# The last projection of the second layer over 33 attention steps in place of 53, and the first output projection over 97 in place of 77

## The chip, the core and the metric

The kernel runs on one core of one Trainium2 chip. The metric is the device time of one execution in microseconds (us). A core has five engines with a queue of instructions each: TensorE (PE, matrix products), VectorE (DVE), ScalarE (ACT), GpSimd (POOL) and SyncE (SP, which here only issues transfers). An engine takes its instructions in the order in which the program lists them, so an instruction whose inputs are late holds everything behind it on that engine. Transfers are issued by SP and ACT, and run on 16 DMA engines.

## The reference, cut to what matters

The model has two layers over 1024 latent tokens with a prefix of 256 context tokens, width 1024. The change lies in the second (odd) layer, where half of the channels go through a convolution module (its output is `oc`) and the other half through neighbourhood attention with 8 heads (its output is `od`):

```python
cv, cgl, cg, dq, dk, dv, dg = split_cols(h_lat @ w_in, ODD_WIDTHS)
x_cv, x_cgl, x_cg, x_dq, x_dk, x_dv, x_dg = split_cols(h_ctx @ w_in, ODD_WIDTHS)
oc = conformer_conv(cv, cgl, cg, dw_w, dw_b, ln_g, ln_b)
def d_row(args):                     # one grid row of 64 queries
    ...
    kk = jnp.concatenate([c_dk, kr], axis=1)
    vv = jnp.concatenate([c_dv, vr], axis=1)
    return gqa_attend(qr[:, :, :, None, :], kk, vv, bias).reshape(bsz, GRID_W, D_W)
y_lat = jnp.concatenate([oc, od * jax.nn.silu(dg)], axis=-1) @ w_out
x_lat = x_lat + g_l[:, None, :] * y_lat
return rms_norm(x_lat, final_g)
```

The output projection `@ w_out` is a sum over eight blocks of 128 input channels: blocks 0 to 3 are `oc`, known before the attention begins, and blocks 4 to 7 are `od`.

## The kernel before, in words

All products are made in three matmuls (`mm3`, L317 to L320): each operand is split into a high part and the remainder, and high x high, high x low and low x high are added up in PSUM. So a projection of 128 output channels over 512 tokens takes 24 matmuls of 512 columns.

**The attention of the second layer** is the generator `attn_gen` (L392), here called `main` (L1504). It has 16 groups of one head and one half of the grid, each with 7 tiles of keys, so 112 items. An item makes a score matmul pair (`st`, L465 and L469), adds a bias on DVE (L474, five of seven tiles), takes the exponential on ACT (L475, L477), splits it on ACT and POOL or DVE (`ph`, `pl`, L296 and L299) and multiplies by the values with three matmuls (`ov`, L409 to L411), three items later. The maxima for the group after next are made in between (`mx`, L1342, L1350). An item takes two steps of the generator, and 12 steps lie before the first item; so step s, counted from 1, begins item (s - 13) / 2. At the beginning of a group its values are loaded (`Vt`), the bias table of the next group (`bs`), and on every second group the keys of the next head (`KAt<-KD`, L361, issued by SP, followed by a copy on ACT, L555, and needed by the maxima).

**Other work is woven between the steps** by `weave` (L495): after the k-th step of `main` it emits as many steps of a second generator, the fill, as keep the two in proportion. `WV` has the number of attention steps for each of the five fills, in this order (L1504 to L1514): `d_proj(2)`, `d_proj(3)`, `out1_part(range(4))`, `out1_part((4, 5, 6), (1,))`, and the first endings.

- `d_proj(i)` (L1167) projects q, k, v and the gate of two heads: ten groups of matmuls in 31 steps, 8 groups of 24 matmuls with 512 columns and two with 256 (matmul rows `p<-hh`, `p<-hc`). Its weights are 16 blocks of 128 KB (`wr<-in_od_d`, issued by SP), each split on ACT and POOL into `wh` and `wl`; its results are stored by SP (`QD`, `KD`, `VD`, `GD`). `d_proj(3)` makes heads 6 and 7, whose first load is made when group 10 begins (item 70).
- `out1_alloc` (L1387), between the two, loads `oc` by eight transfers that ACT issues, and splits it (eight casts on ACT, eight subtractions on DVE). It takes its buffers from `h1`, the input of `d_proj`, as these come free.
- `out1_part(range(4))` (L1437) is the output projection over the blocks 0 to 3: 16 results (8 blocks of 128 outputs times two halves) in 32 steps of six matmuls with 512 columns (rows `po<-oc`). For every pair of outputs it loads four weight blocks (`wr<-in_od_wo`, SP), and for every output two pieces of the layer's input (`xs`, L1405, issued by ACT).

The order on every engine is made when the program is built: a planner takes the instructions that are ready in its own estimate of time, lowest priority number first. The number counts up as instructions are emitted. Two rules set where a fill can stand:

```python
cx.enter_context(later(FL[layer[0]]))              # L502: FL[1] = -98
if lag and len(sts) >= lag:                        # L503
    cx.enter_context(tc.issue_after(sts[-lag].ins))  # L504
next(fill, None)                                   # L505
```

`later(-98)` emits the fill as if 98 instructions earlier. `issue_after(sts[-lag].ins)` lets no matmul of a fill step stand on PE before the first score matmul (L465) of the lag-th latest item that was emitted; it binds PE alone, and not the fill's loads and splits. `LAG = (0, 0, 6, 12)` gives the lag of the first four fills: none for the two projections, 6 for `out1_part(range(4))`, 12 for the part after it.

```python
weave(main, WV[1], d_proj(3), 31, False, True, LAG[1])             # L1506
run(out1_alloc())                                                  # L1507
weave(main, WV[2], out1_part(range(4)), 32, False, True, LAG[2])   # L1508
```

Of the kernel before, what the change touches and what calls it, by code (L numbers as in the profile page):

```python
# [54 lines left out]
MODP = ((), (1, 3, 6))  # L55
FL = (80, -98)
LAG = (0, 0, 6, 12)
WV = (73, 53, 77, 24, 12)
SQ = (0, 1)
EV0 = "e0 c0 f0".split()  # L60
EVS = "e1 c1 e2 f1 c2 f2".split()
# [26 lines left out]
def tile_kernel(ctx: ExitStack, tc: tile.TileContext, a, out):  # L88
# [183 lines left out]
    def run(gen):  # L272

        while True:
            try:
                next(gen)
            except StopIteration as e:
                return e.value
# [45 lines left out]
    def load_w(pool, src, c0, nco, width, bufs, leng=lambda dk: "g", dks=range(DK), rb=WPR):  # L324

        wh, wl = {}, {}
        for dk in dks:
            raw = pool.tile([P, width], F32, tag="wr", name=nm("wr"), bufs=rb)
            raws.append(SY.dma_start(raw[:, :nco], src[dk * P : (dk + 1) * P, c0 : c0 + nco]))
            h = pool.tile([P, width], F32R, tag="wh", name=nm("wh"), bufs=bufs)  # L330
            lo = pool.tile([P, width], F32R, tag="wl", name=nm("wl"), bufs=bufs)
            split(raw[:, :nco], h[:, :nco], lo[:, :nco], "s", leng(dk))
            wh[dk] = h
            wl[dk] = lo
        return wh, wl
# [159 lines left out]
    def weave(main, nmain, fill, nfill, last=True, all_fill=True, lag=0):  # L495

        done = 0
        for k in range(nmain):
            next(main, None)
            while done * nmain < (k + 1) * nfill:  # L500
                with ExitStack() as cx:
                    cx.enter_context(later(FL[layer[0]]))  # L502
# [3 lines that stand above are left out]
                done += 1  # L506
        if all_fill:
            for _ in fill:
                pass
        if last:  # L510
            for _ in main:
                pass
# [586 lines left out]
    with ExitStack():  # L1099
# [287 lines left out]
        def out1_alloc():  # L1387
            for c in range(2):
                ocs.append(bigp.tile([P, 2, 4, 512], F32R, tag="big", name=nm("oc")))
            for c in range(2):  # L1390
                x2.append(bigp.tile([P, DK, 512], F32, tag="big", name=nm("x2")))
                od3.append(pair("od3"))
            for c in range(2):
                for f in range(4):
                    lo = ocs[c][:, 1, f, :]
                    SC.dma_start(lo.bitcast(F32), Oc[:, f, c * 512 : (c + 1) * 512])
                    split(lo.bitcast(F32), ocs[c][:, 0, f, :], lo, "s", OCE)
                yield
# [8 lines left out]
        def od_load(hf):  # L1407
            od[hf] = bigp.tile([P, 2, 3, 512], F32R, tag="big", name=nm("od"))
            for f in range(3):
                lo = od[hf][:, 1, f, :]  # L1410
                SY.dma_start(lo.bitcast(F32), O1d[:, f, hf, :])
                split(lo.bitcast(F32), od[hf][:, 0, f, :], lo, "s", ODE)
# [24 lines left out]
        def out1_part(fs, ks=(0, 1)):  # L1437
            for e2 in range(4):
                w = load_w(wp, a["od_wo"], e2 * 256, 256, 256, WB, dks=fs)
                for e in (2 * e2, 2 * e2 + 1):  # L1440
                    if fs[0] == 0:
                        x2_load(e)
                    for k in ks:
                        yield from out1(fs, e, k, *w)
# [49 lines left out]
        def ends(evs):  # L1494
            for ev in evs:
                k = int(ev[1])
                if ev[0] == "e":
                    yield from out1_end(k)
                elif ev[0] == "c":
                    bcs[k] = yield from rstd_steps(dpool, sums[k], ENDS[k][2], BCT[k])  # L1500
                else:
                    yield from final_norm(k, bcs[k])

        main = attn_gen(dpool, groups1, VSH, LOOK1, {11: [], 12: [13, 14], 13: [15]})  # L1504
        weave(main, WV[0], d_proj(2), 31, False, True, LAG[0])
# [3 lines that stand above are left out]
        assert fin[0] >= 12  # L1509
        for hf in (1, 0):  # L1510
            od_load(hf)
        weave(main, WV[3], out1_part((4, 5, 6), (1,)), 8, False, True, LAG[3])
        assert fin[0] >= 14
        weave(main, WV[4], ends(EV0), NEV, False, True)  # L1514
        wend = [load_w(wp, a["od_wo"], e2 * 256, 256, 256, WB, lambda dk: "gv"[dk % 2], dks=[7]) for e2 in range(4)]
# [118 lines left out]
```

## Time and profile before

| | us |
|---|---|
| three timed runs | 1565.54, 1564.83, 1552.5 (median 1564.83) |
| the profiled execution's own time | 1555.72 |
| its span, first to last instruction | 1553.9 |

The profile is of one execution. A busy time is the sum of the durations of an engine's instructions; matmuls overlap, so that PE looks busier than its array is. PEclk is the granted clock of TensorE, 1.00 being full speed. DMA share is the mean busy share of the 16 DMA engines. Names stand for tiles, as `po<-oc,wh` for a matmul that writes `po` and reads `oc` and `wh`; L numbers are lines of the kernel. In the tables of stretches, the count in brackets is of the instructions that run in a stretch.

### The profile page before, as it was taken

The page shows a single profiled execution, that of the slowest core. Times are in us where ns is not written, and L with a number is a line of the kernel's source. Part 1 is how long each engine was busy: PE and PEld are TensorE (multiplying, and loading weights), DVE is VectorE, ACT ScalarE, POOL GpSimd, SP SyncE. Part 2 cuts the span into 40 slices and gives each one's busy share as a digit, 9 for nine tenths or more (in the row PEclk, how much of TensorE's full clock was granted, in tenths as well). Part 3 has the DMA queues.
Part 4 walks back from the last instruction along what each step waited for, and adds up shares of the span by engine and source line. Part 5 has one row for each costly group of instructions (what it writes and reads, how often), then busy time and mean ns, then how long its engine had stood idle before and what let it go on. Part 6 is the DMA issues. An engine that isn't in the chain of part 4 may idle for free.

```text
span 1553.9 us, 22052 instructions
## 1 busy us (share of the span) xinstructions
PE 1449.1 (93%) x6984; PEld 1172.3 (75%) x6984; DVE 1123.3 (72%) x2172; ACT 759.8 (49%) x1545; POOL 833.5 (54%) x762
## 2 busy tenths in 40 slices
PE   6989989999999989899999889999999999799995
PEld 1878868887789678678887668888787787687784
DVE  4998898689858666654577677999755457586776
ACT  2721354445454755565455555443434455545563
POOL 1561464555555676675455666664542443545574
PEclk9999999999999999999999999999999999899996
DMA  9548245423441124631111121213456888788623
GB/s 339 194 146 270 79 125 174 147 64 121 151 129 44 54 89 143 207 115 56 42 45 35 68 95 57 80 63 123 158 178 222 272 225 263 221 264 240 192 92 109
DMA packets 185614, 221.01 MB, mean 142 GB/s; under 512 B 17421, under 2 KB 139481, under 8 KB 185497
## 3 DMA queue, kind: packets, MB, share of 16 engines
q1 hardware_dynamic: 178832, 208.03, 43.1%
q10 hardware_dynamic: 6664, 11.57, 2.3%
q8 instruction: 55, 0.90, 0.2%
q14 instruction: 63, 0.51, 0.1%
HBM read 159.51 MB, written 60.03 MB: 141 GB/s over the span
## 4 chain that ended last, share of the span: by engine, by line
PE 67%; DVE 12%; DMA 11%; issue 3%; POOL 3%; ACT 2%; SPq 2%; DVEq 0%; ACTq 0%; POOLq 0%
PE p L320 6%; PE p L318 6%; PE p L319 6%; PE ov L409 4%; PE ov L410 4%; PE ov L411 4%; PE st L465 4%; PE po L318 4%; PE st L469 4%; PE po L319 4%; PE po L320 4%; PE pq L320 2%; PE pq L319 2%; PE pq L318 2%; DMA mw<-in_mod_w_dram 2%
## 5 line engine op out<-in xcount | busy, mean ns | idle before, releaser
L299 POOL TENSOR_TENSOR pl<-pf,ph 128x512 fp32r<-128x512 f32 (+4 forms) x321 | 399.9, 1258 | 270.7 <-ACT ph L296 218.9
L299 POOL TENSOR_TENSOR wl<-wr,wh 128x256 fp32r<-128x256 f32 (+2 forms) x256 | 197.7, 788 | 227.9 <-ACT wh L296 203.3
L477 ACT ACTIVATE pf<-st 128x512 f32<-128x512 f32 x284 | 166.2, 596 | 161.7 <-PE st L469 106.3
L296 ACT CAST ph<-pf 128x512 fp32r<-128x512 f32 (+4 forms) x364 | 209.2, 588 | 25.5 <-PE ov L410 17.6
L296 ACT CAST wh<-wr 128x256 fp32r<-128x256 f32 (+2 forms) x264 | 103.2, 404 | 172.2 <-DMA wr<-in_od_d_dram 39.3
L318 PE MATMUL p<-hh,wh 128*128 128x512 f32 x448 | 177.7, 399 | 3.7 <-DVE spk L299 1.4
L319 PE MATMUL p<-hl,wh 128*128 128x512 f32 x448 | 177.9, 398 | 0.2 <-POOL hl L299 0.2
L320 PE MATMUL p<-hh,wl 128*128 128x512 f32 x448 | 175.2, 399 | 0.1
L465 PE MATMUL st<-QH,KAt 128*128 128x512 f32 (+4 forms) x364 | 144.0, 397 | 19.8 <-ACT pf L477 16.5
L409 PE MATMUL ov<-ph,Vt 128*128 128x512 f32 (+4 forms) x364 | 143.6, 394 | 8.8 <-DVE y L631 6.4
L411 PE MATMUL ov<-pl,Vt 128*128 128x512 f32 (+4 forms) x364 | 143.7, 395 | 3.9 <-POOL pl L299 3.8
L410 PE MATMUL ov<-ph,Vt 128*64 128x512 f32 (+4 forms) x364 | 140.8, 387 | 0.0
L469 PE MATMUL st<-QL,KBt 68*128 68x512 f32 (+4 forms) x364 | 138.2, 388 | 0.8 <-DVE QL L388 0.7
L1116 DVE SCALAR_TENSOR_TENSOR cps<-U,taps,cps 128x512 f32<-128x512 f32 x184 | 124.3, 747 | 0.0
L589 DVE TENSOR_REDUCE mp<-mx 128x1 f32<-128x512 f32 x128 | 85.5, 682 | 33.5 <-PE mx L588 32.7
L219 DVE SCALAR_TENSOR_TENSOR macc<-mw,csil,macc 128x512 f32<-128x512 f32 x107 | 97.5, 929 | 14.0 <-DMA mw<-in_mod_w_dram 13.2
L318 PEld LDWEIGHTS p<-hh,wh 128*128 128x128 f32 x448 | 84.6, 189 | 24.5 <-DVE spk L299 1.6
L465 PEld LDWEIGHTS st<-QH,KAt 128*128 128x128 f32 x364 | 69.8, 192 | 42.5 <-ACT pf L477 25.3
L319 PEld LDWEIGHTS p<-hl,wh 128*128 128x128 f32 x448 | 84.6, 189 | 20.4 <-POOL hl L299 0.6
L320 PEld LDWEIGHTS p<-hh,wl 128*128 128x128 f32 x448 | 84.6, 189 | 20.3 <-POOL wl L299 1.0
L411 PEld LDWEIGHTS ov<-pl,Vt 128*128 128x128 f32 x364 | 71.1, 195 | 28.1 <-POOL pl L299 7.6
L409 PEld LDWEIGHTS ov<-ph,Vt 128*128 128x128 f32 x364 | 71.5, 196 | 24.3 <-issue 7.0
(277 smaller groups left out, 3518.4 us busy)
## 6 DMA issues: line engine op xcount, KB each, us to landing
mw<-in_mod_w_dram SPq DMA_DIRECT2D x34, 512.0 KB, 5.6
bs<-in_d_bs_dram SPq DMA_DIRECT2D x16, 832.0 KB, 7.3
Q<-qs SPq DMA_DIRECT2D x40, 256.0 KB, 2.7
QH<-Q SPq DMA_DIRECT2D x80, 128.0 KB, 2.7
bm<-in_d_bm_dram SPq DMA_DIRECT2D x16, 540.0 KB, 6.1
wr<-in_od_d_dram SPq DMA_DIRECT2D x64, 128.0 KB, 2.6
mw<-in_mod_w_dram SPq DMA_DIRECT2D x28, 256.0 KB, 3.1
wr<-in_ev_qkv_dram SPq DMA_DIRECT2D x32, 192.0 KB, 3.8
```

Of the source, the lines that this page charges most:

```text
L296: SC.copy(hi, src)
L299: (GP if leng == "g" else VE).tensor_tensor(lo, src, hi.bitcast(F32), op=ALU.subtract)
L318: PE.matmul(o, lh, rh, start=first, stop=False)
L319: PE.matmul(o, lh, rl, start=False, stop=False)
L320: done[0] = PE.matmul(o, ll, rh, start=False, stop=last)
L409: PE.matmul(o, V[:, 64:192], ph[:, :n], start=(t == 0), stop=False)
L410: PE.matmul(g.ov[0:64, q0 : q0 + n], V[:, 0:64], ph[:, :n], start=False, stop=False)
L411: pvs.append(PE.matmul(o, V[:, 64:192], pl[:, :n], start=False, stop=(last and g.sink is None)))
L465: sts.append(PE.matmul(st[:, :n], KA[:, cs], g.QH[:, q0 : q0 + n], start=True, stop=False))
L469: PE.matmul(st[:, :n], KB[0:68, cs], g.QL[0:68, q0 : q0 + n], start=False, stop=True)
L477: SC.activation(pf[:, :n], st[:, :n], AF.Exp, scale=1.0 if g.bias else SCALE)
L1116: VE.scalar_tensor_tensor(pc, uc, w, pc, op0=ALU.mult, op1=ALU.add)
```

## The change

One line changes: of five numbers in `WV`, the second goes from 53 to 33 and the third from 77 to 97.

```diff
 LAG = (0, 0, 6, 12)
-WV = (73, 53, 77, 24, 12)
+WV = (73, 33, 97, 24, 12)
 SQ = (0, 1)
```

`d_proj(3)` is still emitted from step 74 of the attention, but ends at step 106 in place of 126, 31 fill steps over 33 attention steps. `out1_alloc` follows there, and `out1_part(range(4))` begins at step 107 in place of 127 and ends at step 203 as before, 32 fill steps over 97 attention steps in place of 77. Everything from step 204 on is emitted at the same step as before. No instruction is added or removed; the order on the engines is planned anew.

## The prediction

> **What bounds the kernel now.** I read the page's head first, then the tables of stretches for all instructions and for single tiles, then the timeline of PE, the chain of work that ended last, the waits, and the DMA issues. The head says that PE is the fullest engine; but matmuls overlap, so the array's own load must come from their spacing.
>
> ```profile
> span 1553.9 us, 22052 instructions
> ...
> PE 1449.1 (93%) x6984; PEld 1172.3 (75%) x6984; DVE 1123.3 (72%) x2172; ACT 759.8 (49%) x1545; POOL 833.5 (54%) x762
> ```
>
> The stretch that the change can touch is the second layer's attention while `d_proj(3)` and `out1_part(range(4))` run beside it. Cut where the fill changes, all instructions (us, then each engine's busy time with its count, PEclk, DMA share, GB/s):
>
> ```profile
> core 0: us, PE busy (x) PEld busy (x) DVE busy (x) ACT busy (x) POOL busy (x), PEclk, DMA share, GB/s
> 1237.00:1300.00 63.00, 62.05 (x320) 51.54 (x319) 37.26 (x92) 34.25 (x76) 32.00 (x36) 1.00 0.82 235
> 1300.00:1338.30 38.30, 34.03 (x171) 27.09 (x170) 30.36 (x70) 21.70 (x47) 12.46 (x15) 0.96 0.76 244
> 1338.30:1361.20 22.90, 15.64 (x59) 11.58 (x57) 10.71 (x28) 11.36 (x23) 10.09 (x11) 0.70 0.90 229
> 1361.20:1420.00 58.80, 57.38 (x283) 46.90 (x284) 47.27 (x116) 30.78 (x63) 29.43 (x30) 1.00 0.87 252
> 1420.00:1453.30 33.30, 30.03 (x138) 23.98 (x137) 19.47 (x45) 17.75 (x36) 15.73 (x18) 0.95 0.84 238
> ```
>
> The third row stands out: PE 15.64 of 22.90 us, clock 0.70. The same cuts for the score matmul L465 (PE, weight loads, clock, DMA), one for each item, and for the tiles of the two fills:
>
> ```profile
> 1338.30:1361.20 22.90, 4.48 (x10) 2.31 (x10) 0.70 0.90 229
> 1361.20:1420.00 58.80, 8.90 (x25) 4.71 (x25) 1.00 0.87 252
> ...
> 1338.30:1361.20 22.90, 0.00 (x0) 0.00 (x0) 0.00 (x0) 0.00 (x0) 0.70 0.90 229
> 1361.20:1420.00 58.80, 33.48 (x126) 23.13 (x126) 0.00 (x0) 0.00 (x0) 1.00 0.87 252
> 1420.00:1453.30 33.30, 16.93 (x60) 11.64 (x60) 0.00 (x0) 0.00 (x0) 0.95 0.84 238
> ```
>
> The last three are those of `oc`. So ten items run from 1338.3 to 1361.2 with no fill. The last matmuls of `d_proj(3)`, and the first of the output projection:
>
> ```profile
> L320 PE MATMUL p<-hc,wl x64: 274/281/369, 1084.3 to 1332.2; 128*128 128x256 f32 x64
> ...
> 1338.35 0.40 PE L465 MATMUL st<-QH,KAt 128*128 128x512 f32 x1
> ...
> 1361.22 0.50 PE L465 MATMUL st<-QH,KAt 128*128 128x512 f32 x1
> 1361.55 0.39 PE L469 MATMUL st<-QL,KBt 68*128 68x512 f32 x1
> 1361.78 0.40 PE L318 MATMUL po<-oc,wh 128*128 128x512 f32 x1
> 1362.02 0.40 PE L319 MATMUL po<-oc,wh 128*128 128x512 f32 x1
> 1362.25 0.40 PE L320 MATMUL po<-oc,wl 128*128 128x512 f32 x1
> ```
>
> The projection has run dry at 1332.2, and the next fill starts right behind the score matmul of 1361.22. That is the lag rule: the first step of `out1_part(range(4))` is emitted behind step 127, which begins item (127 - 13) / 2 = 57, so 58 score matmuls exist, the sixth from the end is item 52, and 1361.22 is item 52's. The two 0.40 us matmuls start 0.235 us apart; that is what one of 512 columns costs, and a fill step of six costs 1.41 us.
>
> Now the load of the array. From 1361.2 to 1420 there are 126 x 0.235 = 29.6 us of fill, and with PE busy for 57.38 us at most (57.38 - 29.6) / 25 = 1.11 us for an item of attention. There PE sets the pace: 58.8 / 25 = 2.35 us an item. Without fill an item takes 22.9 / 10 = 2.29 us, nearly the same, though PE needs 1.11: something else sets the pace there. The chain shows it:
>
> ```profile
> 1338.93 10.51 DMA KAt<-KD
> 1349.44 0.02 issue
> 1349.45 3.27 DMA gt<-GD
> ...
> 1354.83 0.43 PE st L465
> 1355.26 0.43 PE st L469
> ...
> 1365.07 0.24 PE po L320
> ```
>
> Transfers hold the chain for 13.8 of 22.9 us, and then PE goes on at half speed, 0.43 where 0.24 is usual. So PE bounds where there is fill, and transfers where there is none.
>
> **The change, part by part.**
>
> *Where the steps go.* The first step of `out1_part(range(4))` comes behind step 107, item 47; the sixth from the end is item 42, whose score matmul is that of 1338.35. The 32 steps then come every 97 / 32 / 2 = 1.52 items in place of 77 / 32 / 2 = 1.20. They still end at items 88 to 89, since both schedules end at step 203. Seven steps (items 42 to 51) move into the empty stretch, 7 x 1.41 = 9.9 us of PE. Per item behind it, fill falls from 29.6 / 25 = 1.18 to 1.41 / 1.52 = 0.93 us.
>
> *`d_proj(3)` emitted more densely.* Its matmuls run far ahead of the rank that emission gives them: step 126 lies in item 56, and the last of them runs before item 42. With 33 steps the last is emitted at item 46, still later than where it runs, so attention that is ready goes first as before. Its 16 weight loads, 16 splits on ACT and POOL and its stores on SP move up in rank alike, past the loads of the groups near item 46 to 56. I take 0. Bounds: PE idles 38.30 - 34.03 = 4.3 us in 1300 to 1338.3, the most to be won; and the ACT casts that wait for weights, first row below, could double, 11.9 us lost. Late next in that case would be the item's exponentials behind them on ACT.
>
> ```profile
> ACT KBt L555 <- DMA KAt<-KD: 13.1, 5, 3.4
> ACT wh L296 <- DMA wr<-in_od_d_dram: 11.9, 7, 4.2
> ...
> L296 ACT CAST oc<-oc x8: 605/616/622, 1307.2 to 1313.0; 128x512 fp32r<-128x512 f32 x8
> L299 DVE TENSOR_TENSOR oc<-oc x8: 648/682/1785, 1310.2 to 1316.8; 128x512 fp32r<-128x512 f32 x8
> 1341.93 0.40 ACT L296 CAST wh<-wr 128x256 fp32r<-128x256 f32 x1 [1.96 <-DMA wr<-in_od_wo_dram]
> 1342.41 0.73 POOL L299 TENSOR_TENSOR wl<-wr,wh 128x256 fp32r<-128x256 f32 x1 [0.98 <-ACT wh L296]
> ```
>
> *`out1_alloc`* is emitted at item 46 in place of 56; its eight casts and subtractions end at 1317, 44 us before their first use, and still 21 us before 1338.35. Nothing on the path; without that cover, 8 x 0.62 on ACT and 8 x 0.68 on DVE, 10 us.
>
> *The empty stretch.* The last of the first four weight blocks is split at 1342.41 + 0.73 = 1343.1, so a first step right behind item 42 could hold PE up to 1343.1 - 1338.6 = 4.5 us; that is the third rival's place. The added transfers, four weight blocks and four input pieces a pair of outputs:
>
> ```profile
> KAt<-KD SPq DMA_DIRECT2D x12, 384.0 KB, 6.9
> xs<-X ACTq DMA_DIRECT2D x16, 256.0 KB, 4.6
> ...
> wr<-in_od_wo_dram SPq DMA_DIRECT2D x14, 128.0 KB, 3.5
> ```
>
> All 32 steps need 16 x 128 + 16 x 256 KB, 192 KB a step; seven are 1.4 MB, 6.0 us at 229 GB/s. The stretch has (1 - 0.90) x 22.9 = 2.3 us of DMA to spare, so it could grow by 3.7 us. The other end: PE needs 11.1 + 9.9 = 21.0 us, at a fill of 57.38 / 58.80 21.5 us, a gain of 1.4. I take a loss of 1, since the chain there is mostly DMA, and a clock kept up gives back half of the five us at 0.43.
>
> The clock: the trace shows PE at 0.70 on average in the one stretch with the longest idle times. The Trainium skill ("TensorE: Matmul & The Clock Gate", What's actually happening) says that half rate is the default and that an idle window of about 3.4 us brings it back. By that rule fill in every item would give back 22.9 x 0.30 = 6.9 us, and the sum would be near the first rival's.
>
> *Items 52 to 76 (1361.2 to 1420).* PE needs 1.11 + 0.93 = 2.04 us an item, at 57.38 / 58.80 2.09 in place of 2.35: 25 x 0.26 = 6.5 us. DMA: 51.2 us busy, less 4.5 steps (0.9 MB, 3.5 us) is 47.7, which at 0.91, the fullest 20 us that I found, is 52.4 us: a gain of 6.4.
>
> ```profile
> 1200.00:1220.00 20.00, 17.49 (x76) 13.08 (x75) 6.07 (x16) 4.94 (x9) 7.02 (x9) 1.00 0.91 295
> ```
>
> Late next are the transfers, and then DVE, 47.27 of 52 us. I take 5 of the 6.5, and 0 is the other end. *Items 77 to 88:* PE idles 3.3 us there already, so it is hardly the bound; fill falls by 12 x 0.25 = 3 us at most, I take 1. Behind step 203 nothing moves.
>
> Sum: 0 + 1 - 5 - 1 = -5 us. Ends: -4.3 - 1.4 - 6.5 - 3 = -15.2, and +11.9 + 3.7 = +15.6. Against the profiled execution, 1555.7, that is 1550.7. The timed runs have 1552.5 to 1565.5, the median 9.1 us over the profiled one; the mean of all four is 1559.7, and 1559.7 - 5 = 1554.7. Between the two, I give 1553.
>
> **The rivals.**
>
> *The clock stays up and PE alone sets the pace.* All gains at their ends: -15.2, 1540 against the profiled run. For it: 0.70 in the empty stretch, and PE full wherever there is fill. Against it: a DMA share of 0.90 with no fill at all. The skill's clock gate, above, speaks for it.
>
> *It does nothing that can be seen.* The transfers alone set the pace from item 42 to 88; they take 0.90 x 22.9 + 0.87 x 58.8 + 0.84 x 33.3 = 99.8 us of 115 wherever the matmuls stand. 1556 to 1560, as before.
>
> *Slower: PE is held by output projection steps that come before their weights.* Its place is the first step of each of the four pairs of outputs. The planner's times are not the chip's; a step put right behind item 42 finds its weights 4.5 us late, and item 43's scores stand behind it on PE, and its exponentials on ACT behind those. For it: `KAt` took 10.51 us there against a median of 6.9. Against: later pairs have 12 items for their loads. Four such waits are 18 us, with the 5 us gained +13, 1569; one alone leaves the forecast's sum near 0. It decides from two late pairs on (9 us over the gain of 6). The Trainium skill ("DMA: Bandwidth & Descriptors", Issuing engines are not separate DMA queues) says that loads from SP and ACT share the same 16 engines, so `xs` would delay `KAt`; the long landing agrees.
>
> **How the numbers follow.** About 1% is what a measurement of this kernel can tell from no change. Forecast 0.45 (0.03 of it beyond 1% at each side); clock and PE alone 0.22, of it 0.17 beyond 1%; nothing seen 0.13; slower 0.20, of it 0.15 beyond 1%. That makes 0.20 faster, 0.62 the same, 0.18 slower. The range goes from 1555.7 - 15.2 = 1540, a little below for the fastest run, 1538, to 1559.7 + 13, 1572.
>
> **What would show it.** First, `po<-oc` must start behind the score matmul of item 42 and go on for 47 items in place of 37; if it starts near 1360 still, the lag rule is not what set it. Second, no ten items without fill, and a clock near 1.00 in that stretch. Third, 2.1 to 2.2 us an item from item 52 on; if 2.35, then transfers or DVE bound there. Long waits of PE for `wh` or `wl` behind item 42 would show the slower rival. A `d_proj(3)` that ends much sooner than before item 42 would break the 0 of its part, since the empty stretch would only move.

## The result and the profile after

| | median (us) | lowest to highest | executions |
|---|---|---|---|
| kernel before | 1558.65 | 1552.5 to 1566.76 | 20 |
| changed kernel | 1566.3 | 1553.51 to 1574.07 | 20 |

The ratio is 1.0039, with a 95% interval of [1.0024, 1.0054]: about 6 us slower (1559 x 0.0024 = 3.7 to 1559 x 0.0054 = 8.4). The forecast was 5 us faster. The time lies in the range of 1538 to 1572, and the move is within 1%, but its sign is the opposite one. The profiled execution of the changed kernel took 1553.51 us, the shortest of its 20, so its total says nothing against the median; its stretches do.

Here is the table of stretches of the changed kernel, cut at the same items as the prediction's: items 42 to 51, 52 to 76, 77 to 88, and 89 to the end. The prediction cut the kernel before at 1420.00, 1 us ahead of its item 77, so the fence behind it has the last three rows of the kernel before, cut at the items. Columns as in the prediction: us, busy time and count of each engine, PEclk, DMA share, GB/s.

```profile
1337.43:1359.60 22.17, 19.95 (x101) 16.25 (x99) 13.83 (x35) 13.20 (x27) 11.97 (x13) 1.00 1.00 284
1359.60:1420.13 60.53, 54.32 (x262) 43.76 (x261) 44.91 (x111) 30.66 (x64) 29.96 (x33) 0.97 0.84 239
1420.13:1445.05 24.92, 24.20 (x118) 19.34 (x117) 17.46 (x43) 13.11 (x26) 9.60 (x11) 1.00 0.92 267
1445.05:1551.70 106.65, 85.17 (x406) 69.78 (x404) 75.34 (x160) 55.52 (x125) 66.82 (x71) 0.88 0.35 113
```

```profile
1361.22:1420.98 59.76, 58.36 (x288) 47.77 (x289) 47.70 (x117) 31.73 (x65) 29.43 (x30) 1.00 0.87 253
1420.98:1453.35 32.37, 29.10 (x133) 23.15 (x132) 19.02 (x44) 16.83 (x35) 15.78 (x18) 0.95 0.84 236
1453.35:1553.90 100.55, 82.86 (x407) 68.98 (x405) 73.03 (x160) 52.32 (x119) 64.98 (x67) 0.88 0.35 115
```

Look at the second row. PE has 262 matmuls where the kernel before had 288, and is busy for 54.3 us in place of 58.4, but 25 items take 60.5 us in place of 59.8: what PE was freed of has become idle time. The third row is 7.5 us shorter than its counterpart and the last 6.1 us longer. Those two belong together: a single long item, with three value products and six matmuls of the output projection's last part, begins before the cut in the kernel before (item 88, 6.2 us) and behind it in the changed one (item 89, 8.1 us). So items 77 to the end have to be read together.

The first matmuls of the moved fill and the end of `d_proj(3)`, in the timeline of PE and in the groups of line L320 of the changed kernel:

```profile
1337.43 0.39 PE L465 MATMUL st<-QH,KAt 128*128 128x512 f32 x1
1337.66 0.40 PE L469 MATMUL st<-QL,KBt 68*128 68x512 f32 x1
1337.90 0.40 PE L318 MATMUL po<-oc,wh 128*128 128x512 f32 x1
1338.14 0.40 PE L319 MATMUL po<-oc,wh 128*128 128x512 f32 x1
```

```profile
L320 PE MATMUL p<-hc,wl x64: 274/281/369, 1082.1 to 1331.3; 128*128 128x256 f32 x64
```

The fill stands right behind item 42's scores, as the lag rule said, without a wait for its weights, and `d_proj(3)` still ends 6 us ahead of item 42.

What PE waited for from item 42 to 1500 us, the total, how often and the longest, in the kernel before and in the changed one:

```profile
PE mx L1342 <- DMA gt<-GD: 3.2, 1, 3.2
PE mx L1342 <- DMA KAt<-KD: 2.8, 1, 2.8
PE st L465 <- DVE pf L474: 2.6, 2, 1.8
PE st L465 <- ACT pf L477: 2.1, 2, 1.8
PE mx L1342 <- DMA QH<-QD: 0.5, 1, 0.5
```

```profile
PE mx L1342 <- DMA QH<-QD: 8.7, 4, 2.3
PE ov L411 <- POOL pl L299: 2.5, 1, 2.5
PE ov L409 <- ACT ph L296: 1.2, 1, 1.2
```

In the kernel before, the wait for `gt` and 1.8 us each of the two for `pf` lie in the empty stretch, and the one for `KAt` at item 87. None of them is left at its size, and a new one has come: four times PE arrives at the row maxima (`mx`) of the group after next before the query load `QH` that they read has landed. (Second profiles of both kernels, below, have 2.0 us of this wait before and 11.2 us after.) The chain of waits of the changed kernel shows one of them: the load lands 7.3 us after its issue, PE stands still, and the maxima start within 0.3 us.

```profile
1369.83 7.30 DMA QH<-QD
1377.13 0.25 issue
1377.38 0.48 PE mx L1342 x2
```

### The profile page after: what moved, and what is told of

Same layout as the page of the kernel before. It is cut to its first block, busy times and chain, and to the rows that moved or that the text cites. A ratio compares the mean times of both kernels' runs of the same rounds, so it can differ in the third digit from the quotient of the medians.

```text
span 1551.7 us, 22050 instructions
## 1 busy us (share of the span) xinstructions
PE 1448.4 (93%) x6984; PEld 1170.8 (75%) x6984; DVE 1124.1 (72%) x2172; ACT 760.8 (49%) x1545; POOL 831.3 (54%) x762
## 4 chain that ended last, share of the span: by engine, by line
PE 66%; DVE 13%; DMA 12%; issue 3%; POOL 2%; ACT 2%; SPq 2%; ACTq 0%; DVEq 0%; POOLq 0%
PE p L320 6%; PE p L319 6%; PE p L318 6%; PE ov L409 4%; PE ov L410 4%; PE ov L411 4%; PE st L465 4%; PE po L318 4%; PE po L320 4%; PE po L319 4%; PE st L469 4%; DMA mw<-in_mod_w_dram 2%; DMA QH<-QD 2%; PE pq L320 2%; PE pg L318 2%
## 5 line engine op out<-in xcount | busy, mean ns | idle before, releaser
L320 PE MATMUL p<-hh,wl 128*128 128x512 f32 x448 | 175.5, 399 | 0.1
L465 PE MATMUL st<-QH,KAt 128*128 128x512 f32 (+4 forms) x364 | 143.6, 396 | 14.2 <-ACT pf L477 12.4
L320 PEld LDWEIGHTS p<-hh,wl 128*128 128x128 f32 x448 | 84.9, 189 | 20.2 <-POOL wl L299 0.6
L465 PEld LDWEIGHTS st<-QH,KAt 128*128 128x128 f32 x364 | 69.4, 191 | 36.2 <-ACT pf L477 20.7
```

What stands on the lines that cost most here:

```text
L320: done[0] = PE.matmul(o, ll, rh, start=False, stop=last)
L465: sts.append(PE.matmul(st[:, :n], KA[:, cs], g.QH[:, q0 : q0 + n], start=True, stop=False))
```

## The experiments

Ratios are to the kernel before, run on the same chip, with 95% intervals. "Items 52 to 83" runs from the score matmul of item 52 to that of item 84. In rows of stretches, the columns are those above.

**The two kernels once more**, for a second profile of each, with no edit.

> The kernel before, unchanged, for a second profile of it. Theory (the tail gives it back): items 42 to 88 take 108 to 112 us and items 89 to the end about 101 us, as in the first profile (108.8 from 1338.4 to 1447.2 and 106.7 from there to the end). Rival (the clock): the time differs between executions mostly by how long TensorE runs at half clock (105 us of it in the first profile), and the second profile shows that in the same places.

> The changed kernel, unchanged, for a second profile: its first one, 1553.5, is the fastest of 20 executions with a median of 1566.3, so it does not show what the usual one loses. Theory (transfers): the usual execution is 10 to 15 us longer between items 42 and 89, where key and query loads are waited for (in the first profile query loads 11.2 us, key copies 10.9 us); these waits grow to 30 us or more together. Rival (the tail): items 42 to 88 are as short as in the first profile (105.9 us), and the 10 us lie behind item 89, at the waits for the od blocks. Second rival (the clock): over 110 us at half clock in place of 97.

One execution each: 1561.65 and 1568.3 us. With these, and with place_only below, the stretches are (differences of the starts of L465 in the timelines, to the end of the span for the last; us):

| | before | before, again | changed | changed, again | place_only |
|---|---|---|---|---|---|
| start of item 42 | 1338.4 | 1347.6 | 1337.4 | 1346.7 | 1347.4 |
| items 42 to 51 | 22.9 | 19.7 | 22.2 | 25.7 | 21.1 |
| items 52 to 76 | 59.8 | 61.1 | 60.5 | 63.1 | 61.7 |
| item 77 to the end | 132.9 | 131.5 | 131.6 | 131.0 | 134.2 |
| item 42 to the end | 215.6 | 212.2 | 214.3 | 219.8 | 217.0 |

Ahead of item 42 executions of one kernel differ by 9 us, and the change shows nothing there. Behind it the changed order takes 217.0 us in the mean, and the kernel before 213.9. That is 3 us of the 6 that the timed runs show, and less than the 5.5 us by which two executions of the changed kernel differ.

**The placing alone.** The kernel before, with each step of `out1_part(range(4))` bound on PE to the item where the changed kernel has it, and the emission as it was:

```diff
-                    if lag and len(sts) >= lag:
+                    if isinstance(lag, list):
+                        cx.enter_context(tc.issue_after(sts[252 + lag[done]].ins))
+                    elif lag and len(sts) >= lag:
...
-        weave(main, WV[2], out1_part(range(4)), 32, False, True, LAG[2])
+        weave(main, WV[2], out1_part(range(4)), 32, False, True, [(94 + 97 * j // 32) // 2 - 5 for j in range(32)])
```

> The kernel before, with every step of the first output projection allowed on TensorE from the item where the changed kernel allows it (items 42 to 88 in place of 52 to 89); the emission of the last projection and of the first output projection, and so the ranks of their loads, stay as before. Theory (the placing on TensorE is all that the change does): same as the changed kernel, 1.002 to 1.006 of before. Rival (the denser emission of the last projection, or the earlier rank of the loads, costs the time): 0.995 to 1.000.

1570.15 us, 1.0050 [1.0027, 1.0074]. Items 42 to 51, 52 to 76 and 77 to 88 of its trace hold 42, 102 and 48 matmuls of `po<-oc`, exactly as in the changed kernel (0, 126 and 60 in the kernel before). So the place of the projection's matmuls on PE is enough for the whole loss; emitting `d_proj(3)` and `out1_alloc` earlier neither gains nor costs anything that the intervals can tell (1.0039 with it, 1.0050 without).

**The last part of the output projection held back** (`LAG[3]` 6 in place of 12 in the changed kernel), and **its input split on VectorE** in place of GpSimd (`ODE`):

```diff
-LAG = (0, 0, 6, 12)
+LAG = (0, 0, 6, 6)
```

```diff
-OCE, ODE, OHE = ('v', 'g', 'g')
+OCE, ODE, OHE = ('v', 'v', 'g')
```

> The changed kernel with the lag of the second part of the output projection (blocks 4 to 6) at 6 in place of 12, so that its first step may not stand on TensorE before item 90 (it stands behind item 87 in the changed kernel). Known by now: items 42 to 88 are 0 to 7 us shorter than before, items 89 to 104 are 8 to 9 us longer (49 to 52 in place of 41.5). Theory (order: the od steps and splits that stand ahead of items 88 to 90 hold them): items 89 to 104 fall to 42 to 45 us, the whole to 0.996 to 1.000 of before. Rival (transfers: what item 93 needs cannot land sooner, so what is won earlier is waited for here): unchanged within 2 us, 1.003 to 1.006.

> The changed kernel with the low parts of the od blocks made by VectorE in place of GpSimd. In the changed kernel GpSimd waits 3.1 us at item 89 for an od block, and the low part of the attention's weights, which TensorE waits 2.5 us for, stands behind it. Theory (order, and on GpSimd): the stretch from item 89 to 104 is 3 to 6 us shorter than the changed kernel's 49 to 52, the whole 0.999 to 1.002 of before. Rival (transfers): 1.003 to 1.006.

1574.82 us, 1.0084 [1.0055, 1.0112], and 1572.71 us, 1.0082 [1.0059, 1.0105]. Both are slower than the changed kernel (1.0039), and items 89 to 104, which were to get shorter, take 49.4 and 50.4 us, beside 50.5 and 49.3 in the two profiles of the changed kernel. So neither the early matmuls of `od` nor its split on GpSimd is what costs, and both theories fell. What makes these two slower is open.

**Fewer transfers.** The bias tables are loaded for the first six groups only, and later groups use those again (so their bias is another head's); 8.3 MB of transfers go.

```diff
             def load_bs():
+                if gi >= 6:
+                    for t in range(5):
+                        bss[t] = kept[hf][t]
+                    return
+                kept[hf] = bss
```

> The kernel before, with the bias tables (832 KB a group) loaded for the first six groups alone; the other ten use those of groups 4 and 5, so their bias is another head's. 8.3 MB of transfers are gone, all from item 35 on, 33 us of transfer time at 250 GB/s. Theory (transfers bound this stretch): 10 to 25 us faster than before, 0.984 to 0.994. Rival (order on the engines): 0 to 4 us faster, 0.997 to 1.000.

> The changed kernel with the same bias loads left out. Theory (transfers take back what the change wins): with transfers relieved it is 4 us or more faster than its partner, the kernel before without these loads. Rival (order): 4 to 8 us slower than that partner, as with all loads.

1561.47 us, 1.0009 [0.9989, 1.0029], and 1558.84 us, 0.9993 [0.9976, 1.0009]. The volume of transfers bounds neither order. Here are items 52 to 83 of the changed kernel, first as it is, then with the fewer loads:

```profile
1359.60:1433.65 74.05, 67.39 (x326) 54.04 (x325) 55.08 (x135) 37.90 (x78) 36.14 (x39) 0.98 0.84 240
```

```profile
1368.44:1444.52 76.08, 68.17 (x324) 53.78 (x322) 54.63 (x135) 37.89 (x78) 35.12 (x38) 0.98 0.65 187
```

The DMA share goes from 0.84 to 0.65, and the stretch is no shorter. Nor is the empty stretch of the kernel before, items 42 to 51, which has 22.9 us in the prediction. Here it is in the second profile, and with the fewer loads:

```profile
1347.58:1367.24 19.66, 15.23 (x60) 11.13 (x58) 10.95 (x28) 11.28 (x23) 9.33 (x11) 0.74 0.98 257
```

```profile
1349.85:1372.60 22.75, 16.09 (x66) 12.11 (x64) 13.33 (x33) 11.79 (x24) 9.45 (x10) 0.79 0.70 180
```

It is shortest where the DMA share is highest. Yet by the timed runs the changed order no longer loses beside its partner (the table below). In the list of transfers of 1337 to 1475 us, a query load lands after 4.2 us in the median where it took 7.1, so the lateness of single loads came under suspicion. This is theory Q of the next expectations: the changed order loses because PE reaches the maxima before the query loads.

**A fourth pair of query buffers**, so that the load can be issued a group earlier:

```diff
-        QH = pool.tile([P, 512], F32R, tag="QH", name=nm("QH"), bufs=3)
-        QL = pool.tile([P, 512], F32R, tag="QL", name=nm("QL"), bufs=3)
+        if g.extra_q is None:
+            QH = pool.tile([P, 512], F32R, tag="QH", name=nm("QH"), bufs=3)
...
+        else:
+            QH = g.extra_q.tile([P, 512], F32R, tag="QHx", name=nm("QH"), bufs=1)
...
+            g = Group(extra_q=dpool if gi % 4 == 3 else None, load_q=load_q, maxes=maxes, nmp=2, bias=True, rate=3, ahead=ahead, sink=None, tiles=tiles, den=den, finish=finish,
```

> The kernel before with a fourth pair of query buffers in the second layer (every fourth group's QH and QL come from the other pool), so that a group's query load can be issued about a group earlier. Theory Q (the changed order loses because PE reaches the row maxima before the query load that they need has landed): in the kernel before, PE waits only 0.5 to 2.0 us on query loads behind item 42, so there is little to win: ratio to the kernel before 0.997 to 1.001. Rival (buffers have nothing to do with it; the changed order loses by something else): also 0.999 to 1.002. This run is the partner of the next one.

> The changed kernel with the same fourth pair of query buffers. Theory Q: the 7 to 11 us in which PE waits on query loads in items 42 to 105 fall below 2, items 89 to the end come back from 106 us to some 101, and the time is no longer above that of its partner: ratio to the kernel before 0.994 to 1.000. Rival (the loads only stand where the delay shows, the loss comes from the order of the fill on PE as such): the ratio stays at 1.003 to 1.006, as without the buffers, with PE's idle time put down to something else.

1562.92 us, 1.0022 [1.0001, 1.0042], and 1562.7 us, 1.0036 [1.0013, 1.0059]. PE's waits in the second, from item 42 to 1500 us:

```profile
PE st L469 <- ACT pf L481: 3.0, 1, 3.0
PE ov L415 <- POOL pl L299: 2.7, 2, 2.4
PE mx L1346 <- DMA KAt<-KD: 2.4, 1, 2.4
```

The wait for `QH` is gone from the list, and against the kernel before nothing is clearly won: other waits stand in its place, one after the other (`pf`, `pl`, `KAt`). Beside the partner, which got slower too, the loss is too small to be told from nothing. So this pair decides neither for theory Q nor fully against it.

**The maxima later**: one item, then two.

```diff
-LEAD = (3, 4)
+LEAD = (3, 5)
```

> The changed kernel with the row maxima of the second layer started one item later (LEAD 5 in place of 4), everything else as it is. Theory Q: a query load then has about 2 us longer to land before PE asks for it, so the waits on it fall from 9 to 11 us to about half, and the ratio to the kernel before falls from 1.004 to 0.999 to 1.002. Rival: no effect or slower, 1.003 to 1.008, since the maxima are then later for the group that needs them.

> The changed kernel with the row maxima started two items later (LEAD 6). Theory Q: about 4 us longer for each load, the waits all but vanish (below 3 us), ratio 0.997 to 1.002 unless the later maxima make the next group's subtraction of them late, which would show as a wait at the first item of a group. Rival: 1.004 to 1.010.

> The kernel before with the row maxima of the second layer started one item later, partner of lead5_after (1.0011). If the later maxima are worth 1 to 3 us in any order, the ratio is 0.998 to 1.000 and the change still costs 0.2 to 0.3% beside it; if they are worth something only where the fill is thinner (theory Q: in the kernel before PE waits at most 2 us on query loads), the ratio is 1.000 to 1.003 and the change costs nothing beside this partner.

1560.43 us, 1.0011 [0.9989, 1.0032]; 1561.79 us, 1.0020 [1.0001, 1.0040]; and for the partner 1561.32 us, 1.0004 [0.9989, 1.0020]. PE's waits for `QH` fall from 8.7 to 3.8 us in the first:

```profile
PE mx L1342 <- DMA QH<-QD: 3.8, 2, 2.1
PE ov L409 <- DVE y L1367: 3.3, 2, 2.1
```

By the timed runs the later maxima take back most of what the change lost and do nothing for the kernel before, as theory Q said. The traces do not bear out its reason. Here are PE's waits for `QH` from item 42 to 1500 us in lead5_before, few_bias_before and few_bias_after, in this order:

```profile
PE mx L1342 <- DMA QH<-QD: 6.3, 3, 3.4
```

```profile
PE mx L1347 <- DMA QH<-QD: 6.8, 4, 3.7
```

```profile
PE mx L1347 <- DMA QH<-QD: 4.3, 2, 2.4
```

Two kernels with the order from before wait for query loads for 6.3 and 6.8 us, longer than their changed partners (3.8 and 4.3), and are no slower than the kernel before, which waits for 0.5 and 2.0 us (1.0004 and 1.0009). So what PE waits for these loads is not what the time goes by. Nor is the gain of lead5_after seen behind item 42: there it takes 217.6 us, beside 214.3 and 219.8 in the two profiles of the changed kernel.

**Is PE the bound of items 52 to 83 at all?** The kernel before without the two low-order products of the first output projection:

```diff
-                mm3(pp, wh[f][:, es], wl[f][:, es], hi, lo, j == 0, j == len(fs) - 1)
+                if fs[0] == 0:
+                    PE.matmul(pp, wh[f][:, es], hi, start=j == 0, stop=j == len(fs) - 1)
+                else:
+                    mm3(pp, wh[f][:, es], wl[f][:, es], hi, lo, j == 0, j == len(fs) - 1)
```

> The kernel before with the two low-order products of the first output projection left out: 128 of its 192 matmuls of 0.235 us (30 us of PE's work) are not issued, loads, splits and everything else stay. The output loses those products. Theory that a second bound stands just behind PE: items 52 to 83 stay at 71 to 76 us although some 100 matmuls (24 us) are gone, PE's idle time takes their place, ratio 0.995 to 1.000. Rival, PE alone sets the pace there: items 52 to 83 fall to 55 to 60 us, ratio 0.986 to 0.990. If idle time brings the clock down, the granted clock of the stretch shows it.

1564.36 us, 1.0026 [1.0005, 1.0048]. The two rows are items 52 to 83 of the kernel before and of this one:

```profile
1361.22:1436.33 75.11, 73.56 (x362) 60.12 (x362) 58.09 (x141) 40.69 (x84) 39.09 (x41) 1.00 0.85 248
```

```profile
1366.25:1442.61 76.36, 59.78 (x253) 43.50 (x254) 57.85 (x141) 39.93 (x83) 38.22 (x40) 0.91 0.85 246
```

This is the run that settles most. 109 matmuls are gone, PE is busy for 14 us less, and the stretch takes 76.4 us, as it does in the second profile of the kernel before (1367.24 to 1443.64). A PE that is busy for 73.6 of 75.1 us looked like the bound and is not the only one: much of the work that fills it is fill, and what is under the fill takes the same 75 to 76 us. (The clock is 0.91 here in place of 1.00, which takes part of what could be won; 0.09 of the busy time is an estimated 5 us, of 14.)

**A third `pf` buffer.** Each item's scores are in `pf` from VectorE's add until both splits have read them, and there are two of these buffers. Theory P of the next expectations is that these two buffers set the pace there. In items 52 to 83 VectorE's add waits for the second split, in the kernel before and in the changed one:

```profile
DVE pf L474 <- POOL pl L299: 7.1, 5, 2.5
```

```profile
DVE pf L474 <- POOL pl L299: 8.3, 7, 2.4
```

```diff
-            pf = pool.tile([P, 512], F32, tag="pf" if layer[0] else "ost", name=nm("pf"), bufs=PFB)
+            pf = pool.tile([P, 512], F32, tag="pf" if layer[0] else "ost", name=nm("pf"), bufs=3 if layer[0] else PFB)
```

> The changed kernel with three score buffers (pf) in the second layer in place of two. Theory P (behind item 52 a second chain stands within 1 us of PE: add, exp and the two splits of a score tile hold its pf buffer some 4 us, two buffers give one item in about 2.2 us, so PE's 6 us less work in items 52 to 83 became idle time): the 8 us in which VectorE's pf add waits on GpSimd's pl in that stretch fall below 3, items 52 to 83 fall from 74 to 77 us to 68 to 72, and the ratio to the kernel before falls from 1.004 to 0.996 to 1.000. Theory Q (only the query loads matter): PE's waits on them stay at 7 to 11 us and the ratio at 1.002 to 1.006.

> The kernel before with three score buffers in the second layer. Theory P: PE is busy for 73.6 of 75.1 us in items 52 to 83, so a faster second chain brings at most 1 to 2 us there and a little in items 42 to 51: ratio 0.997 to 1.001. If the score chain were the first bound here too, the ratio would be 0.992 to 0.996. Partner of the run before it.

1557.84 us, 0.9977 [0.9957, 0.9996], and 1556.4 us, 0.9975 [0.9954, 0.9996]. With three buffers the change costs nothing that the intervals can tell, and the wait for `pl` is gone from VectorE's list for the changed kernel. Its items 52 to 83 take 71.0 us:

```profile
1358.32:1429.36 71.04, 65.46 (x308) 52.90 (x307) 51.32 (x128) 37.23 (x78) 35.25 (x39) 0.95 0.86 249
```

What was not expected is that the partner gains as much, and that both gain ahead of the moved fill. Items 30 to 41 of pfb3_before, beside 37.9 and 39.0 us in the two profiles of the kernel before:

```profile
1308.18:1339.09 30.91, 29.96 (x154) 24.16 (x152) 26.43 (x57) 20.07 (x43) 9.82 (x9) 1.00 0.80 239
```

That is 7 us or more, and in pfb3_after the same items take 30.7 us in place of 38.9 and 40.2. Behind item 42 part of it is given back: pfb3_before takes 219.2 us from there to the end, beside 215.6 and 212.2 (its items 52 to 83 take 81.3), and pfb3_after 218.8, beside 214.3 and 219.8.

**Both at once**: the low-order products left out, and three buffers.

> thin_before (the low-order products of the first output projection left out) with three score buffers. Theory P (the two score buffers are the second bound): with PE's load gone and the buffers free, items 52 to 83 fall from 76.4 to 65 to 71 us and the ratio to the kernel before from 1.0026 to 0.990 to 0.996. If the pace there is set by something else (the maxima with VectorE's reductions, and the loads that these wait for), the stretch stays at 73 to 78 us, the ratio at 0.998 to 1.002, and only the gain of the buffers ahead of item 42 (some 7 us in items 30 to 41 of pfb3_before) is seen, against a lower clock.

1551.09 us, 0.9926 [0.9900, 0.9953]. Items 52 to 83:

```profile
1358.64:1424.37 65.73, 52.59 (x239) 38.40 (x237) 55.01 (x138) 38.59 (x81) 37.73 (x41) 0.95 0.95 283
```

65.7 us where two buffers gave 76.4, with the same work left out. So it is the two `pf` buffers that hold these items at 75 us and more when PE has less to do. How they do it is not shown: in thin_before no wait of VectorE's add for `pl` is left in its list, so it may be by the order that the planner lays out for two buffers rather than by a wait for one. The same 30 us of matmuls taken off PE cost 0.3% with two buffers and bring 0.5% with three (0.9926 against 0.9975).

**Both loosened.** Three `pf` buffers and the maxima one item later, in both orders (the last two diffs together).

> The changed kernel with three score buffers and the row maxima one item later. If the two loosen different chains, their effects add to those of pfb3_after (0.9977) and lead5_after (1.0011 against 1.0039): 0.994 to 0.998, the best kernel of the study. If they loosen the same slack, the ratio stays at 0.997 to 1.000.

> The kernel before with three score buffers and the row maxima one item later, partner of the run before it. If the change is neutral once the score buffers are no longer tight (pfb3_after 0.9977 and pfb3_before 0.9975), the two partners agree within 0.2%: 0.995 to 0.999. If the changed order wins as soon as both chains are loose, this one is slower than its partner by 0.3% or more.

1559.83 us, 0.9987 [0.9970, 1.0005], and 1553.1 us, 0.9948 [0.9928, 0.9968]. The second is the best kernel of this study that computes the whole reference, some 8 us ahead of the kernel before, and it has the order from before. Items 42 to 51 and 52 to 83, changed order first:

```profile
1333.01:1361.08 28.07, 24.48 (x132) 19.68 (x131) 17.21 (x46) 14.59 (x34) 13.50 (x16) 1.00 0.97 285
1361.08:1435.30 74.22, 65.41 (x312) 52.13 (x311) 54.95 (x134) 37.84 (x78) 36.52 (x40) 0.95 0.83 236
```

```profile
1333.90:1351.95 18.05, 15.64 (x88) 11.93 (x87) 16.02 (x41) 13.12 (x31) 10.90 (x13) 1.00 0.98 291
1351.95:1430.60 78.65, 73.58 (x360) 59.39 (x358) 58.75 (x140) 40.59 (x86) 41.80 (x45) 1.00 0.89 256
```

In the order from before the empty stretch takes 18.1 us here, at full clock, with two buffers 22.9 and 19.7. The steps that the change puts there cost 10.0 us, and only 4.4 come back by item 83; behind it the changed order is another 3.8 us longer. One profile each cannot say how the 6.1 us (0.0039 of 1560) between the two ratios divide. PE's waits for `QH` from item 42 to 1490 us are 7.4 us in the changed order against 3.5.

Changed order over its partner, from the ratios (half width: root of the sum of the squares of both):

| loosened | changed / partner |
|---|---|
| nothing | 1.0039 ± 0.0015 |
| bias loads | 0.9984 ± 0.0026 |
| query buffers | 1.0014 ± 0.0031 |
| maxima by one item | 1.0007 ± 0.0027 |
| `pf` buffers | 1.0002 ± 0.0029 |
| `pf` buffers and maxima | 1.0039 ± 0.0027 |

No version of the changed order is ahead of its partner beyond the interval. With buffers and maxima loosened together the loss is back at its full size, so neither of the two is shown to be what costs, though each alone seemed to remove the loss.

## Why the prediction was wrong, point by point

**Where the steps go: right.** Item 42 is where the fill begins, and it needs no weights that are late. The slower rival, PE held for `wh` or `wl` behind item 42, did not happen: no such wait stands in the list of PE's waits of the changed kernel.

**`d_proj(3)` and `out1_alloc` at 0: right, within the intervals.** place_only, which leaves both where they were, is as slow as the changed kernel.

**The empty stretch at +1: about right.** 22.2, 25.7 and 21.1 us stand against 22.9 and 19.7, 1.7 more in the mean. The clock is at 1.00 there in the changed kernel and in place_only, and at 0.93 in the second profile, against 0.70 and 0.74 before. The Trainium skill ("TensorE: Matmul & The Clock Gate", What's actually happening) says that half rate is the default and that activity lifts it; the trace agrees. The 6.9 us that the prediction worked out from it did not come. The one wait of PE that is listed in these ten items is for `QH`, 2.2, 4.4 and 1.5 us; for the rest, 20.0, 21.3 and 19.7 us, PE is busy, near the 21.0 that the prediction had as PE's own need. What the clock alone was worth is not shown. The 1 came out near by luck: its reason was the transfers, and with fewer of them the stretch was no shorter.

**"There PE sets the pace" and "I take 5 of the 6.5" in items 52 to 76: the step that failed.** 60.5, 63.1 and 61.7 us stand against 59.8 and 61.1: +1.3 in the mean in place of -5. PE's load did fall, but the time did not follow. The prediction had read the bound from PE's busy time, 57.38 of 58.80 us, and had then worked out two followers, the transfers at 52.4 us and VectorE at 47. Both were busy times of resources. What is next behind PE is no resource that is full. Items 52 to 83 need some 76 us even where PE has 14 us less to do (thin_before), and 65.7 with a third `pf` buffer (thin_pfb3_before). So the steps that share the two buffers (add, exponential, two splits), or the order that two buffers force on the engines, stand close behind PE. The prediction had a hint of it in hand: the ten items with no fill took 2.29 us each, "nearly the same" as the 2.35 with fill (2.39 when cut at item 77). It put that to the transfers of that stretch; few_bias_before shows that transfers by volume do not bound it, 22.75 us at a DMA share of 0.70. In the second profile it is 1.97 us against 2.44, so that comparison alone would have been a weak one.

**Items 77 to 88 at -1, and "behind step 203 nothing moves": right in their sum.** From item 77 to the end the kernels take 132.9 and 131.5 us before, 131.6, 131.0 and 134.2 after. Part by part they are off: items 77 to 88 are 6.7 us shorter in the mean and the rest 6.8 us longer, since what runs ahead of item 88 moves behind it though nothing there is emitted otherwise.

**The sum.** +1.7, +1.3 and 0 make +3 us in the profiles; the timed runs say +6, between 3.7 and 8.4. Why it is more than 0 stays open. What is shown is that the place of the fill's matmuls is enough for it (place_only). In the three traces of that placing PE waits for query loads for 8.7, 11.2 and 9.1 us, and later maxima or fewer loads took most of the loss away in the timed runs (lead5_after, few_bias_after). But the partners of these two wait for the same loads for 6.3 and 6.8 us and lose nothing, q4_after is without the wait and did not clearly get faster, and with three `pf` buffers and later maxima together the loss is back. So the late query loads go with the loss and are not shown to be its cause.

**The rivals.** "It does nothing that can be seen" came nearest, if barely, with the wrong reason: it named the transfers. The slower one had the right side, but its late weights did not come. It had also set the upper end of the range, so that the time lies inside is luck. That a resource's fullness was taken for the pace is what all the cases with a gain had in common.

**What would show it.** The first two signs came as written. The third, 2.1 to 2.2 us an item, came out at 60.53 / 25 = 2.42. For such a number the prediction had named transfers or VectorE as the bound. Transfers by volume it is not (few_bias_after), and VectorE is busy for 44.9 of the 60.5 us.

## What to carry to other kernels

An engine that is filled with movable work looks like the bound wherever that work stands; ask how long the stretch takes without it, best from a run that leaves most of it out, before a gain is counted for taking some away. Here that run left the stretch at 76.4 us. A stretch where the fill is missing is a hint only: here 2.29 us an item against 2.35 in one profile, 1.97 against 2.44 in another. Then loosen what stands behind the engine first: the same matmuls left out were worth nothing with two `pf` buffers and 0.5% with three. And a wait that a list shows on the engine is no price: two kernels with 4 to 6 us more of the wait for query loads took the same time.

## What the runs showed that was not expected

- Leaving out 109 of 362 matmuls in a stretch left it at 76.4 us (75.1 and 76.4 with them), at a granted clock of 0.91 in place of 1.00.
- 8.3 MB fewer transfers took the DMA share of items 52 to 83 from 0.84 to 0.65, and left that stretch no shorter (76.1 us after 74.1); but a 128 KB query load landed after 4.2 us in the median in place of 7.1.
- Executions of one program reached item 42 at 1338.4 and at 1347.6 us; so single profiles of this kernel are better compared by stretch than by total, and even a stretch differed by 3 us (22.9 and 19.7).
